# Two projection parts per attention unit, earlier exponentials, and a last residual kept in PSUM: a two-layer hybrid decoder trunk

## The chip, the cores and the metric

The kernel runs on one core of one Trainium2 chip. A core has five engines that run their own queues in order: TensorE (PE) for matrix products, VectorE (DVE), ScalarE (ACT), GpSimd (POOL) and SyncE (SP), which here only issues transfers. An engine that must wait for another stops at the waiting instruction, and everything behind it in its queue waits as well. The metric is the device time of one execution in microseconds; for several executions it is their median.

## The reference, cut to what matters

One sequence of 256 tokens, width 1024, all in float32. Layer 0 is a gated DeltaNet, layer 1 a sparse attention with three branches (compressed, selection, window), and each ends in a residual sum and a LayerNorm:

```
x  = layer_norm(alpha * x + gated_deltanet(x))          # layer 0
kv = six key/value projections of x, two of them compressed by a small MLP
q, z, gates = x @ b_w_in                                # 1024 + 3072 + 48 columns
o  = sum over 3 branches of gate * softmax(q k^T) v * silu(z)    # 16 heads of 64
x  = layer_norm(alpha * x + o @ b_w_out)                # layer 1, the output
```

With 256 tokens all blocks are selected and the window covers everything, so the selection and window branches are two causal softmaxes over 256 keys, and the compressed branch is one over 15 blocks.

## The kernel before, in words

All weights stream from HBM as tiles of 128x1024 into a ring of five raw buffers. ACT casts each one to a rounded high half (`hi_...`, L181) and POOL takes the difference as a low half (`lo_...`, L185); eight pairs can be held. A product is then three matmuls: high times high, high times low, low times high (L233 to L235). A **part** is six such matmuls of 512 columns: one weight tile against one half of the tokens (t = 0 or 1). Parts of the z projection write `pbz`, those of the output projection `pbo` (tokens 0 to 127) and `pbl` (tokens 128 to 255).

The order on PE, DVE, ACT and POOL is the order in which the Python code writes the instructions. Parts stand in a list `fills`, and `fill(n)` writes the next n of them. `defer(k, f)` puts work off until `step()` has been called k times; each `fill` of one part calls `step()` first. When the fourth part of a group of 512 z columns is written, its follow-up is deferred by one step: a tanh on ACT (`th`, L1236), then the multiplication with z on DVE (`zz<-th,pbz`, L1237). `get` and `presplit` write the casts of tiles that will be needed later.

The attention is a loop over 24 **units**, numbered 0 to 23 here. A unit of t = 0 is two heads for tokens 0 to 127; a unit of t = 1 is one head for tokens 128 to 255. The string `UNITS` gives their order. Each pass writes, in this order: `scores` (four matmuls into one of two PSUM tiles `s`), `maxima` (DVE adds the mask and reduces: L1345 to L1347 for t = 0, L1349 to L1352 for t = 1), `probs` of the unit before (ACT copies its transposed exponentials out of PSUM: `PT`, L1385, and `PcT`, L1389), `FA[i]` parts, one pending `merge`, `presplit`, `exps` (ACT, L1365 and L1366, or L1369 and L1370), `readout` of the unit before (PE, L1404, L1407, L1410, into the one PSUM tile `op`), `FB[i]` parts, and `transposes` (PE, L1378, into the one PSUM tile `ptp`, and L1380). The follow-up of a readout, `total` (five DVE instructions, L1418 to L1422), is deferred by one step and writes the gated sum into `zz`. For a unit of t = 0, `maxima` stands ahead of `probs` and `step`:

```
        first = i < n and units[i][0] == 0 and not merges
        if first:
            maxima(units[i])
```

`merge` transposes finished sums (PE `tp_b`, L1436; ACT `x1h`, L1440; DVE `x1l`, L1441), after which parts of the output projection can be written. `gates` (one ACT instruction, four DVE instructions, L1310 to L1315) works in place in a PSUM tile that is one of the two buffers of `s`, and is deferred to the first unit. The queries are split and transposed ahead of the loop: `q_split` (ACT and DVE, L1047 and L1048), `q_post` (PE `qtp`, L1223) and a deferred ACT copy to `qT` (L1224); the last of these transposes uses the PSUM buffer of `ptp`.

At the end, `done` adds the residual for tokens 128 to 255 in four quarters of 256 columns (`ln_part`, L914 and L915) and `ln_affine` normalises: `ln_mean` on DVE and POOL (L921 to L923), two DVE instructions that subtract the mean and multiply by the weight (L939), two that scale and add the bias (L942), each followed by a store.

Of the kernel before, what the change touches and what calls it, by code (L numbers as in the profile page):

```python
# [13 lines left out]
ALU = mybir.AluOpType  # L14
# [7 lines left out]
SQRT2 = float((2.0 * 2) ** 0.25)  # L22
# [12 lines left out]

FIRST = (1, 2)

UNITS = "001010101101101101111111"
FA = "3113111011210212044211123"
FB = "0211121311122110212111000"  # L40

PRE, TAIL = 4, 2
NEG = -1e30
# [50 lines left out]
def trunk(ctx: ExitStack, tc: tile.TileContext, I: dict, out: bass.AP):  # L94
    nc = tc.nc
    V, S, G, PE = nc.vector, nc.scalar, nc.gpsimd, nc.tensor
# [7 lines left out]
    def defer(n, f):  # L104
        late.append([n, f])

    def step():
        for e in late:
            e[0] -= 1
        due = [e for e in late if e[0] <= 0]  # L110
        late[:] = [e for e in late if e[0] > 0]
        for _, f in due:
            f()
# [82 lines left out]
    def lower():  # L196
        while lows:
            lows.pop(0)()
# [42 lines left out]
    def presplit():  # L241
        oldest = next(i for i, n in enumerate(uses) if n)
        split_to(min(state["top"] + PRE, oldest + NSPL, state["s"] + 1))
        lower()

    def fill(n, low=True):
        for _ in range(n):
            step()
            if fills:
                fills.pop(0)()  # L250
            if low:
                lower()
# [25 lines left out]
    first = ring.tile([P, 1024], F32, tag="raw", name="raw_first", bufs=NRAW)  # L278
    raws[order[0]] = first
    state["l"] = 1  # L280
    for q in range(4):
        if q in FIRST:
            c = slice(FIRST.index(q) * 512, FIRST.index(q) * 512 + 512)
# [48 lines left out]
    for q in range(5):  # L332
        if q < 4:
            c = slice(2 * q, 2 * q + 2)
# [223 lines left out]
    lo, hi = slice(0, 64), slice(64, 128)  # L558
# [233 lines left out]
    lnp = {}  # L792
# [115 lines left out]
    def ln_part(t, w, lo, ps, xin, dst):  # L908

        if lo == 0:  # L910
            stt[w, t] = [sm.tile([P, 4, 6], F32, tag="st", name=f"st_{w}{t}"), 0]
        st, n = stt[w, t]
        cc = slice(lo, lo + ps.shape[-1])
        V.scalar_tensor_tensor(dst[:, cc], xin[:, cc], SQRT2, ps, op0=ALU.mult, op1=ALU.add)  # L914
        V.bn_stats(st[:, n, :], dst[:, cc])  # L915
        stt[w, t][1] += 1

    def ln_mean(t, w):
# [6 lines left out]

    def ln_affine(t, w, b, dst, store=None, src=None):
        mv = ln_mean(t, w)
        if src:

            for c in range(2):  # L930
                V.scalar_tensor_tensor(src[c], src[c], mv[:, 0:1], lnp[w][:, c * 512:c * 512 + 512],
                                       op0=ALU.subtract, op1=ALU.mult)
            for c in range(2):
                cc = slice(c * 512, (c + 1) * 512)
                V.scalar_tensor_tensor(dst[:, cc], src[c], mv[:, 1:2], lnp[b][:, cc], op0=ALU.mult, op1=ALU.add)
            return
        for c in range(2):
            cc = slice(c * 512, (c + 1) * 512)
            V.scalar_tensor_tensor(dst[:, cc], dst[:, cc], mv[:, 0:1], lnp[w][:, cc], op0=ALU.subtract, op1=ALU.mult)  # L939
        for c in range(2):  # L940
            cc = slice(c * 512, (c + 1) * 512)
            V.scalar_tensor_tensor(dst[:, cc], dst[:, cc], mv[:, 1:2], lnp[b][:, cc], op0=ALU.mult, op1=ALU.add)  # L942
            if store:
                store(cc)

    def ln_affine_aside(t, w, b, dst, store):

        mv = ln_mean(t, w)
        nb = sm.tile([P, 1], F32, tag="nb", name=f"nb_{w}{t}")
        V.scalar_tensor_tensor(nb, mv[:, 0:1], -1.0, mv[:, 1:2], op0=ALU.mult, op1=ALU.mult)  # L950

        def half(c):
            cc = slice(c * 512, (c + 1) * 512)
            S.activation(dst[:, cc], dst[:, cc], AF.Identity, bias=nb, scale=mv[:, 1:2])
            G.tensor_tensor(dst[:, cc], dst[:, cc], lnp[w][:, cc], op=ALU.mult)
            G.tensor_tensor(dst[:, cc], dst[:, cc], lnp[b][:, cc], op=ALU.add)
            store(cc)

        defer(1, lambda: half(0))
        defer(3, lambda: half(1))  # L960
# [171 lines left out]
    for a in range(2):  # L1132
        for gp in range(2):
            step()
            ps = proj_fm(("skv", 2 * a + gp), x1h, x1l, f"pc{a}{gp}")
# [122 lines left out]
    add_pairs(48)  # L1258
    S.copy(wgs[:, :, 0:48], wg)
    G.tensor_tensor(wgs[:, :, 48:96], wg, wgs[:, :, 0:48].bitcast(F32), op=ALU.subtract)  # L1260
    fill(1)
    r = q_split()
    fill(1)
    compressed_v()
    for i in range(4):
        if i:
# [8 lines left out]
    for c in range(6):  # L1275
        for t in range(2):
            k = len(fills)
# [44 lines left out]
    order1 = [(1, h) for h in range(16)]  # L1322
    units = [order0.pop(0) if k == "0" else order1.pop(0) for k in UNITS]
    S_, PT_, PTT, PC, PCT, MX, TP = {}, {}, {}, {}, {}, {}, {}
# [29 lines left out]
    def exps(u):  # L1354
        t, h = u
        sp, mx = S_[u], MX[u]
        s4 = sp[:, :, 0:256].rearrange("p j (b k) -> p j b k", b=2)
        pt = PT_[u] = wk.tile([P, 2, 2, P], F32, tag="hl", name=f"pt{t}{h}", bufs=3)
        if t == 0 or h % 2 == 0:
            PC[t, h] = wk.tile([P, 2, 16], F32, tag="Pc", name=f"Pc{t}{h}", bufs=4)  # L1360
        Pc = PC[t, h - h % 2]
        if t == 0:
            for j in range(2):
                for b in range(2):
                    S.activation(pt[:, j, b, :], s4[:, j, b, :], AF.Exp, bias=mx[:, 2 * j + b:2 * j + b + 1])  # L1365
                S.activation(Pc[:, j, :], sp[:, j, 256:272], AF.Exp, bias=mx[:, 4 + j:5 + j])  # L1366
        else:
            for b in range(2):
                S.activation(pt[:, :, b, :], s4[:, :, b, :], AF.Exp, bias=mx[:, b:b + 1])  # L1369
            S.activation(Pc[:, h % 2, :], sp[:, 0, 256:272], AF.Exp, bias=mx[:, 4:5])  # L1370
# [11 lines left out]
    def probs(u):  # L1382
        t, h = u
        PT = PTT[u] = wk.tile([P, 2, 2, P], F32, tag="ra", name=f"PT{t}{h}", bufs=6)
        S.copy(PT.rearrange("p a b c -> p (a b c)"), TP[u])  # L1385
        if t == 0 or h % 2:
            h -= h % 2 * t
            PCT[t, h] = pct[len(PCT) % 2]
            S.copy(PCT[t, h][0:32, :], S_[u][0:32, 1, 272:400])  # L1389
# [39 lines left out]
    pb_ = {}  # L1429
# [13 lines left out]
    def bo_unit(t, c, part):  # L1443
        if part == 0:
            pb_[t, c] = [(sbank(f"pbl{c}{f}")[:, 0] if c else pjb(f"pbl{c}{f}")) for f in range(2)] if t else pjb(f"pbo{c}{t}")
        if t == 0 and c == 1 and part == 1:
            for nm in ("blw", "blb"):
                load_ln(nm, ring.tile([P, D], F32, tag="raw", name=nm, bufs=NRAW))
        x = x1[:, t, :]

        def store(cc):
            nc.sync.dma_start(out[t * P:(t + 1) * P, cc], x[:, cc])

        def done(lo, ps):
            ln_part(t, "blw", lo, ps, x, x)
            if lo + ps.shape[-1] == D:
                (ln_affine if t else ln_affine_aside)(t, "blw", "blb", x, store)

        if t == 1:

            for f in range(2):
                ps = pb_[t, c][f][:, 0:256]
                tm_part(ps, ("bo", 4 * c + part), part, t, *bT, cols=slice(256 * f, 256 * f + 256))
                if part == 3:
                    done(512 * c + 256 * f, ps)
            return
        tm_part(pb_[t, c], ("bo", 4 * c + part), part, t, *bT)
        if part == 3:
            defer(1, lambda: done(512 * c, pb_[t, c]))
# [5 lines left out]
    merges, ready = [], []  # L1475
    cnt["t0"] = 0

    def advance():
        if merges:
            merges.pop(0)()  # L1480
# [13 lines left out]
    n = len(units)  # L1494
    for i in range(n + 1):
        if i < n:
            scores(units[i])
        first = i < n and units[i][0] == 0 and not merges
        if first:

            maxima(units[i])
        if i:
            probs(units[i - 1])
        step()
        if i < n and not first:
            maxima(units[i])
        fill(int(FA[i]))
        advance()
        presplit()
        if i < n:  # L1510
            exps(units[i])
        if i:
            t, h = units[i - 1]
            if t == 0:
                readout(t, h)
                if h == 14:
                    cnt["t0"] = 1
                    merges += [lambda: merge0(0), lambda: merge0(1)] + ready
            else:

                if (units[i - 2] if h % 2 else units[i]) == (1, h ^ 1):
                    readout(t, h - h % 2, h % 2)
                elif h % 2:
                    readout(t, h - 1)
                if h % 4 == 3:
                    (merges if cnt["t0"] else ready).append(lambda g_=h // 4: merge1(g_))
        fill(int(FB[i]))
        if i < n:
            transposes(units[i])
# [79 lines left out]
```

## Time and profile before

| | |
|---|---|
| median of 3 runs | 386.9 us (386.45 to 387.45) |
| profiled execution, its own time | 388.53 us |
| profiled execution, span from first to last instruction | 386.8 us |
| PE busy | 374.7 us, 97% of the span |
| DVE, ACT, POOL busy | 58%, 57%, 64% |
| matrix products end at | about 379 us |

The profiled execution took 1.7 us more than its span and 1.6 us more than the median of the runs. Times in rows count from the start of the span. A row of a timeline gives the start, the length, the engine, the line, the operation, the output and inputs, the shapes, how many instructions it stands for, and in brackets how long the engine had been idle and on whom it waited. A matmul's length overlaps that of the next one, so the work of PE is read from the distance between two starts.

### The profile page before, as it was taken

The numbers are of one execution on the slowest core, as the hardware profiler recorded it, in microseconds if no ns is written. First come the engines' busy times: TensorE is split into PE (matmuls) and PEld (weight loads), VectorE is DVE, ScalarE is ACT, GpSimd is POOL, SyncE is SP. The second block draws the span as 40 slices with busy tenths as digits, with TensorE's granted clock in tenths as the row PEclk, the third lists the DMA queues.
The fourth block names the chain that finished last, engine by engine and source line by source line (L and its number), as shares of the span: only waits on it lengthen the run. The fifth ranks groups of instructions, "written<-read, shape, count | busy, mean of one in ns | idle before, by whom it ended". The sixth has DMA issues, their size and how long they took to land.

```text
span 386.8 us, 7558 instructions
## 1 busy us (share of the span) xinstructions
PE 374.7 (97%) x2870; PEld 332.9 (86%) x2870; DVE 223.6 (58%) x591; ACT 220.4 (57%) x433; POOL 247.1 (64%) x157
## 2 busy tenths in 40 slices
PE   8899999999999999999999999999999999999991
PEld 6899999999888987888897878888888888878991
DVE  2777876588642543656542545754557456677726
ACT  4687785546854543535563567675664757456410
POOL 5499999837456747895854997474736547209051
PEclk9999999999999999999999999999999999999997
DMA  6776749845433316384545854433516143301011
GB/s 223 292 218 208 268 158 297 228 167 143 148 109 112 110 54 200 128 287 147 169 158 166 297 195 159 164 111 109 173 45 218 55 153 113 117 3 54 3 54 54
DMA packets 23476, 58.68 MB, mean 152 GB/s; under 512 B 6672, under 2 KB 9232, under 8 KB 23312
## 3 DMA queue, kind: packets, MB, share of 16 engines
q1 hardware_dynamic: 23232, 58.13, 45.1%
q8 instruction: 22, 0.36, 0.4%
q14 instruction: 14, 0.11, 0.1%
q10 hardware_dynamic: 144, 0.07, 0.1%
q0 software_dynamic: 64, 0.01, 0.0%
HBM read 55.96 MB, written 2.23 MB: 150 GB/s over the span
## 4 chain that ended last, share of the span: by engine, by line
PE 90%; DMA 3%; DVE 2%; POOL 1%; ACT 1%; issue 1%; POOLq 0%; SPq 0%; DVEq 0%
PE pbz L235 6%; PE pbz L233 6%; PE pbz L234 6%; PE op L1407 4%; PE s L1336 3%; PE ptp L1378 3%; PE pwz L233 2%; PE pk L217 2%; PE pwo L235 2%; PE pq L216 2%; PE pq L215 2%; PE pq L217 2%; PE pk L215 2%; PE pk L216 2%; PE pwo L234 2%; PE pwo L233 2%
## 5 line engine op out<-in xcount | busy, mean ns | idle before, releaser
L185 POOL TENSOR_TENSOR lo_bz<-raw_bz,hi_bz 128x1024 fp32r<-128x1024 f32 x24 | 56.8, 2392 | 36.2 <-ACT hi_bz L181 19.6
L185 POOL TENSOR_TENSOR lo_wqkv<-raw_wqkv,hi_wqkv 128x1024 fp32r<-128x1024 f32 x22 | 52.5, 2406 | 7.9 <-ACT hi_wqkv L181 6.1
L233 PE MATMUL pbz<-hi_bz,x1h 128*128 128x512 f32 x96 | 38.7, 403 | 0.0
L235 PE MATMUL pbz<-lo_bz,x1h 128*128 128x512 f32 x96 | 37.8, 394 | 0.0
L234 PE MATMUL pbz<-hi_bz,x1l 128*128 128x512 f32 x96 | 37.6, 392 | 0.0
L185 POOL TENSOR_TENSOR lo_bo<-raw_bo,hi_bo 128x1024 fp32r<-128x1024 f32 x8 | 18.9, 2387 | 21.7 <-ACT hi_bo L181 16.9
L185 POOL TENSOR_TENSOR lo_skv<-raw_skv,hi_skv 128x1024 fp32r<-128x1024 f32 x12 | 28.4, 2397 | 4.2 <-PE pskv L235 4.2
L185 POOL TENSOR_TENSOR lo_wz<-raw_wz,hi_wz 128x1024 fp32r<-128x1024 f32 x8 | 19.4, 2438 | 16.0 <-ACT hi_wz L181 10.6
L181 ACT CAST hi_bz<-raw_bz 128x1024 fp32r<-128x1024 f32 x24 | 25.3, 1052 | 2.5 <-POOL wgs L1260 1.6
L185 POOL TENSOR_TENSOR lo_bq<-raw_bq,hi_bq 128x1024 fp32r<-128x1024 f32 x8 | 19.1, 2393 | 11.6 <-ACT hi_bq L181 7.2
L185 POOL TENSOR_TENSOR lo_wo<-raw_wo,hi_wo 128x1024 fp32r<-128x1024 f32 x8 | 18.9, 2385 | 11.9 <-ACT hi_wo L181 11.9
L1385 ACT COPY PT<-ptp 128x512 f32<-128x512 f32 x24 | 14.1, 588 | 21.2 <-PE ptp L1378 21.2
L181 ACT CAST hi_wqkv<-raw_wqkv 128x1024 fp32r<-128x1024 f32 x22 | 22.8, 1043 | 2.4 <-DMA raw_wqkv<-in_wqkv 2.4
L235 PEld LDWEIGHTS pbz<-lo_bz,x1h 128*128 128x128 f32 x96 | 18.0, 188 | 4.3 <-POOL lo_bz L185 0.2
L234 PEld LDWEIGHTS pbz<-hi_bz,x1l 128*128 128x128 f32 x96 | 18.1, 188 | 2.8
L233 PEld LDWEIGHTS pbz<-hi_bz,x1h 128*128 128x128 f32 x96 | 18.1, 188 | 2.8
L1369 ACT ACTIVATE pt<-s,mx 128x256 f32<-128x256 f32 x32 | 13.4, 471 | 10.9 <-DVE mx L1352 8.7
L217 PE MATMUL pk<-xh,lo_wqkv 128*128 128x256 f32 x64 | 18.2, 285 | 0.9 <-POOL lo_wqkv L185 0.9
L215 PE MATMUL pk<-xh,hi_wqkv 128*128 128x256 f32 x64 | 18.6, 290 | 0.0
L215 PE MATMUL pq<-xh,hi_wqkv 128*128 128x256 f32 x64 | 18.5, 289 | 0.0
L216 PE MATMUL pk<-xl,hi_wqkv 128*128 128x256 f32 x64 | 18.1, 283 | 0.0
L217 PE MATMUL pq<-xh,lo_wqkv 128*128 128x256 f32 x64 | 18.1, 283 | 0.0
(362 smaller groups left out, 1257.9 us busy)
## 6 DMA issues: line engine op xcount, KB each, us to landing
raw_bz<-in_bz SPq DMA_DIRECT2D x24, 512.0 KB, 3.3
raw_wqkv<-in_wqkv SPq DMA_DIRECT2D x23, 512.0 KB, 4.4
raw_skv<-in_skv SPq DMA_DIRECT2D x12, 512.0 KB, 3.3
raw_wz<-in_wz SPq DMA_DIRECT2D x8, 512.0 KB, 3.9
raw_wo<-in_wo SPq DMA_DIRECT2D x8, 512.0 KB, 3.6
raw_bq<-in_bq SPq DMA_DIRECT2D x8, 512.0 KB, 3.6
raw_bo<-in_bo SPq DMA_DIRECT2D x8, 512.0 KB, 3.3
raw_w<-in_w SPq DMA_DIRECT2D x4, 512.0 KB, 3.3
```

What stands on the lines that cost most here:

```text
L181: S.copy(h, r)
L185: e.tensor_tensor(l, r, h.bitcast(F32), op=ALU.subtract)
L215: PE.matmul(ps[:, 0:T], wh[:, kt, :], ah[:, kt, :], start=kt == 0, stop=False)
L216: PE.matmul(ps[:, 0:T], wh[:, kt, :], al_[:, kt, :], start=False, stop=False)
L217: PE.matmul(ps[:, 0:T], wl[:, kt, :], ah[:, kt, :], start=False, stop=kt == 7)
L233: PE.matmul(ps, ah[:, kt, tt], wh[:, k4, cols], start=kt == 0, stop=False)
L234: PE.matmul(ps, al_[:, kt, tt], wh[:, k4, cols], start=False, stop=False)
L235: PE.matmul(ps, ah[:, kt, tt], wl[:, k4, cols], start=False, stop=kt == 7)
L1336: PE.matmul(sp[:, j, 0:n], lq, kk[:, hh // 4, c0:c0 + n], start=i == 0, stop=i == 1)
L1369: S.activation(pt[:, :, b, :], s4[:, :, b, :], AF.Exp, bias=mx[:, b:b + 1])
L1385: S.copy(PT.rearrange("p a b c -> p (a b c)"), TP[u])
L1407: PE.matmul(o3[:, r, 1 + b, :], PT[:, j, b, :], vt_[:, b, j, g_, :], start=j == 0, stop=j == 1)
```

## The change

The tables that order the units and place the parts are rewritten: every unit has one part behind its scores and one behind its readout almost everywhere, where before some had none and some four. For units of t = 0 the exponentials are now written right behind `probs`, ahead of `step()`. For the others they are written ahead of `presplit`. Where a merge is pending, one of the parts behind the scores is now written after the merge. `q_split` for the first group of queries stands one part earlier. In the last LayerNorm the residual sums of columns 0 to 511 stay in PSUM, so the first pass has three instructions, two of 256 columns that read PSUM and one of 512.

```diff
-UNITS = "001010101101101101111111"
-FA = "3113111011210212044211123"
-FB = "0211121311122110212111000"
+UNITS = "001101100111011100111111"
+FA = "3112121111111111111222223"
+FB = "0111111111111111101001000"
...
-        V.scalar_tensor_tensor(dst[:, cc], xin[:, cc], SQRT2, ps, op0=ALU.mult, op1=ALU.add)
-        V.bn_stats(st[:, n, :], dst[:, cc])
+        y = ps if dst is None else dst[:, cc]
+        V.scalar_tensor_tensor(y, xin[:, cc], SQRT2, ps, op0=ALU.mult, op1=ALU.add)
+        V.bn_stats(st[:, n, :], y)
...
-        for c in range(2):
-            cc = slice(c * 512, (c + 1) * 512)
-            V.scalar_tensor_tensor(dst[:, cc], dst[:, cc], mv[:, 0:1], lnp[w][:, cc], op0=ALU.subtract, op1=ALU.mult)
+        for c, y in enumerate(src):
+            cc = slice(c * 256, (c + 1) * 256)
+            V.scalar_tensor_tensor(dst[:, cc], y, mv[:, 0:1], lnp[w][:, cc], op0=ALU.subtract, op1=ALU.mult)
+        cc = slice(512, 1024)
+        V.scalar_tensor_tensor(dst[:, cc], dst[:, cc], mv[:, 0:1], lnp[w][:, cc], op0=ALU.subtract, op1=ALU.mult)
...
-    fill(1)
     r = q_split()
-    fill(1)
+    fill(2)
...
+            inb = t == 1 and lo < 512
+            ln_part(t, "blw", lo, ps, x, None if inb else x)
...
+        if first:
+            exps(units[i])
         step()
         if i < n and not first:
             maxima(units[i])
-        fill(int(FA[i]))
+
+        k = 1 if merges else 0
+        fill(int(FA[i]) - k)
         advance()
+        fill(k)
+        if i < n and not first:
+            exps(units[i])
         presplit()
-        if i < n:
-            exps(units[i])
```

Three places show how instructions move. In the names, digits behind `s`, `mx`, `pt`, `op` are t and the head (`pt014` is t = 0, heads 14 and 15), those behind `th` and `pbz` are the group of columns and t. The lines of the changed kernel are two or three higher.

ACT at unit 0, before:

```order
L181 CAST hi_bz_6_3049<-raw_bz_6_2908 128x1024
L1224 CAST qT1_2696<-qtp110_3059 128x4x128
L1224 CAST qT1_2696<-qtp111_3064 128x4x128
L1310 ACT_TABLE_LOAD
L1310 ACTIVATE gq_3069<-gq_3069 128x96
L181 CAST hi_bz_7_3090<-raw_bz_7_2935 128x1024
L1236 ACTIVATE th00_3101<-pbz00_3004 128x512
L1365 ACTIVATE pt00_3117<-s00_3072,mx00_3077 128x128 x2
```

The same place on ACT in the changed kernel:

```order
L181 CAST hi_bz_6_3049<-raw_bz_6_2908 128x1024
L1367 ACT_TABLE_LOAD
L1367 ACTIVATE pt00_3081<-s00_3072,mx00_3077 128x128 x2
L1368 ACTIVATE Pc00_3082<-s00_3072,mx00_3077 128x16
L1367 ACTIVATE pt00_3081<-s00_3072,mx00_3077 128x128 x2
L1368 ACTIVATE Pc00_3082<-s00_3072,mx00_3077 128x16
L1227 CAST qT1_2696<-qtp110_3059 128x4x128
L1227 CAST qT1_2696<-qtp111_3064 128x4x128
L1312 ACTIVATE gq_3069<-gq_3069 128x96
```

The table load and the exponentials of unit 0 moved ahead of the last two query copies and of the gates.

DVE around the last unit of t = 0 (heads 14 and 15), before, where it is unit 16:

```order
L1237 SCALAR_TENSOR_TENSOR zz3_3808<-th41_3993,pbz41_3896 128x512
L1345 TENSOR_TENSOR s014_4030<-s014_4030,cb_2284 128x2x272
L1346 TENSOR_REDUCE mx014_4035<-s014_4030 128x4
L1347 TENSOR_REDUCE mx014_4035<-s014_4030 128x2
L1418 RECIPROCAL op16_4014<-op16_4014 128x6
```

The same on DVE in the changed kernel, where it is unit 17, from the maxima of unit 16 on:

```order
L1347 TENSOR_TENSOR s012_3962<-s012_3962,cb_2284 128x2x272
L1348 TENSOR_REDUCE mx012_3967<-s012_3962 128x4
L1349 TENSOR_REDUCE mx012_3967<-s012_3962 128x2
L1240 SCALAR_TENSOR_TENSOR zz1_3560<-th50_3982,pbz50_3878 128x512
L1420 RECIPROCAL op18_3945<-op18_3945 128x6
L1421 TENSOR_TENSOR rc18_4003<-op18_3945,gt_2977 128x6
L1422 TENSOR_TENSOR op18_3945<-op18_3945,zz3_3869 128x6x64
L1423 TENSOR_TENSOR op18_3945<-op18_3945,rc18_4003 128x6x64
L1424 TENSOR_REDUCE zz3_3869<-op18_3945 128x128
L1347 TENSOR_TENSOR s014_4021<-s014_4021,cb_2284 128x2x272
```

A total of unit 16, and the multiplication with z ahead of it, now stand in front of the maxima of unit 17.

ACT at the second merge of t = 0, before:

```order
L1385 COPY PT110_4167<-ptp110_4157 128x512
L1440 CAST x1h_2043<-tp_b04_4174 128x4x128
L1369 ACTIVATE pt111_4181<-s111_4162,mx111_4169 128x2x128 x2
L1370 ACTIVATE Pc110_4137<-s111_4162,mx111_4169 128x16
L181 CAST hi_bo_4_4191<-raw_bo_4_3922 128x1024
```

The same merge on ACT in the changed kernel, in unit 20:

```order
L1387 COPY PT111_4185<-ptp111_4174 128x512
L1391 COPY PcT1_2389<-s111_4134 32x128
L1442 CAST x1h_2043<-tp_b04_4199 128x4x128
L1239 ACTIVATE th51_4206<-pbz51_4116 128x512
L181 CAST hi_bo_4_4210<-raw_bo_4_3992 128x1024
L1371 ACTIVATE pt112_4220<-s112_4180,mx112_4188 128x2x128 x2
```

A tanh and a cast moved ahead of the exponentials.

## Rows read from the trace of the kernel before

**Rows 1.** The page: busy time of the engines, share of the span and instructions

```profile
PE 374.7 (97%) x2870; PEld 332.9 (86%) x2870; DVE 223.6 (58%) x591; ACT 220.4 (57%) x433; POOL 247.1 (64%) x157
```

**Rows 2.** Timeline of PE and ACT where the first queries are transposed

```profile
222.23 0.39 PE L234 MATMUL pbq<-hi_bq,x1l 128*128 128x512 f32 x1
222.46 0.39 PE L235 MATMUL pbq<-lo_bq,x1h 128*128 128x512 f32 x1
223.38 0.66 PE L1223 MATMUL qtp<-ident,hlq 128*128 128x128 f32 x4 [0.54 <-DVE hlq L1048]
...
221.55 1.06 ACT L181 CAST hi_bz<-raw_bz 128x1024 fp32r<-128x1024 f32 x1 [1.56 <-POOL wgs L1260]
```

**Rows 3.** Timeline of PE at the merges: transposes of unit 17, then the next output part

```profile
337.56 0.91 PE L1378 MATMUL ptp<-ident,pt 128*128 128x128 f32 x4
...
343.54 0.66 PE L1436 MATMUL tp_b<-ident,zz 128*128 128x128 f32 x4 [0.19 <-ACT PT L1385]
...
345.51 0.48 PE L233 MATMUL pbo<-hi_bo,x1h 128*128 128x512 f32 x1
```

**Rows 4.** Timeline of PE in unit 1, and the first maximum of unit 2

```profile
247.41 1.00 PE L1404 MATMUL op<-vtok,PT 128*128 128x65 f32 x8
...
248.25 0.44 PE L1410 MATMUL op<-vbd,PcT 128*128 128x130 f32 x2
...
251.30 0.60 PE L1378 MATMUL ptp<-ident,pt 128*128 128x128 f32 x4
...
251.77 0.37 PE L1336 MATMUL s<-kh,qT 128*128 128x272 f32 x1
...
252.53 0.43 DVE L1349 TENSOR_TENSOR s<-s,cb 128x256 f32<-128x256 f32 x1 [1.01 <-PE s L1336]
```

**Rows 5.** Timeline of DVE, ACT and PE in units 16 and 7 of t = 0

```profile
331.14 0.73 DVE L1345 TENSOR_TENSOR s<-s,cb 128x544 f32<-128x544 f32 x1 [3.01 <-PE s L1336]
...
332.81 0.62 ACT L1365 ACTIVATE pt<-s,mx 128x128 f32<-128x128 f32 x2 [1.59 <-DVE op L1418]
...
334.33 0.28 PE L1380 MATMUL s<-ident,Pc 128*32 128x128 f32 x1
...
285.30 0.63 ACT L1236 ACTIVATE th<-pbz 128x512 f32<-128x512 f32 x1
...
285.96 0.69 DVE L1237 SCALAR_TENSOR_TENSOR zz<-th,pbz 128x512 f32<-128x512 f32 x1 [2.11 <-ACT th L1236]
```

**Rows 6.** Timeline of DVE: the first and the last of the five instructions of a total

```profile
273.57 0.20 DVE L1418 RECIPROCAL op<-op 128x6 f32<-128x6 f32 x1 [1.83 <-PE op L1410]
...
275.21 0.56 DVE L1422 TENSOR_REDUCE zz<-op 128x128 f32<-128x384 f32 x1
```

**Rows 7.** Timeline of ACT, DVE and PE at unit 0, and an earlier table load

```profile
239.68 1.07 ACT L1224 CAST qT<-qtp 128x512 fp32r<-128x512 f32 x2 [0.20 <-PE qtp L1223]
240.78 1.28 ACT L1310 ACT_TABLE_LOAD   x1
...
242.55 0.26 DVE L1311 TENSOR_SCALAR gq<-gq 128x96 f32<-128x96 f32 x1
...
243.93 0.24 DVE L1315 TENSOR_SCALAR gt<-gq,cb 128x16 f32<-128x16 f32 x1
...
244.98 0.60 PE L1378 MATMUL ptp<-ident,pt 128*128 128x128 f32 x4
...
20.01 1.28 ACT L471 ACT_TABLE_LOAD   x1 [0.54 <-DVE cv L465]
```

**Rows 8.** Instructions of L922 and L923 (ns min/median/max, first and last start), timeline of DVE

```profile
L922 POOL TENSOR_SCALAR mv_blw<-mv_blw x2: 222/500/778, 366.5 to 380.4; 128x1 f32<-128x1 f32 x2
...
L923 POOL TENSOR_TENSOR mv_blw<-mv_blw,mhalf x2: 572/748/925, 366.8 to 381.3; 128x1 f32<-128x1 f32 x2
...
380.39 1.42 DVE L939 SCALAR_TENSOR_TENSOR x<-x,mv_blw,blw 128x512 f32<-128x512 f32 x2
382.26 1.42 DVE L942 SCALAR_TENSOR_TENSOR x<-x,mv_blw,blb 128x512 f32<-128x512 f32 x2 [0.46 <-POOL mv_blw L923]
```

More of the change, by code (lines that the diff above doesn't have):

```diff
@@ L927, in ln_affine @@
         mv = ln_mean(t, w)
-        if src:
+        if src and not store:
             for c in range(2):
@@ L1454, in done @@
         def done(lo, ps):
-            ln_part(t, "blw", lo, ps, x, x)
+            inb = t == 1 and lo < 512
+            ln_part(t, "blw", lo, ps, x, None if inb else x)
             if lo + ps.shape[-1] == D:
-                (ln_affine if t else ln_affine_aside)(t, "blw", "blb", x, store)
+                if t:
+                    ln_affine(t, "blw", "blb", x, store, [p[:, 0:256] for p in pb_[1, 0]])
+                else:
+                    ln_affine_aside(t, "blw", "blb", x, store)
         if t == 1:
```

## The prediction

> **What bounds the kernel now.** The page comes first: PE is busy for 374.7 of 386.8 us [rows 1], so the others matter only where PE waits for them, and after its last matmul. Next come the distances between starts on PE in the stages that the change touches, because modelled ends hide waits. A matmul of 512 columns follows the one before by 0.23 us [rows 2], so a part of six is 1.38 us. Wherever PE's distances equal this work, nothing can be won; three places are longer. At the first transposes of queries PE stands until DVE has split them [rows 2]. At the merges, the stretch from the transposes of unit 17 to the next output part is 7.95 us [rows 3]. After the matmuls come the residual sums and the last normalisation, where DVE waits 0.46 us for POOL [rows 8]. All else that PE does in these stages is the same before and after, since the change only reorders it.
>
> **What it removes.**
> Queries: the split waits in ACT's queue behind a cast of 1.06 us that itself waits for POOL [rows 2]. After the change it stands ahead of that cast. Without the wait the transposes would start at 222.46 + 0.23 = 222.69 instead of 223.38: 0.69 us. The profile calls 0.54 of it idle; I take 0.69, and 0.54 is the lower bound.
>
> Merges: the work in those 7.95 us is two sets of transposes (0.47 and 0.44), two of scores (0.58 each), two merges of four transposes (0.44 each), and readouts of 16, 2 and 8 matmuls (1.68, 0.28, 0.84). These lengths come from unit 1: eight matmuls of a readout 0.84, transposes and the small one behind them 0.47, a readout with its last pair and two parts 3.89, which leaves 0.28 for the pair [rows 4]; scores are what remains of 244.98 to 247.41 after 0.47 and a part [rows 7, 4]. The sum is 5.75, so 2.2 us are waits: no part stood there to cover the totals and copies. In the changed kernel a part stands ahead of each merge and one behind it. With some tenths at single transposes around it I take 2.5, between 1.5 and 2.7.
>
> Last normalisation: the two small POOL instructions took 778 and 925 ns there, and 222 and 572 ns at the other call [rows 8], 0.91 more. DVE was then working through L939, whose operands are all in SBUF; after the change its first two instructions read PSUM. L939 to L942 is 1.87 us; two instructions of 256 columns and one of 512 need about 1.5, and POOL's 0.8 fits inside. So at most 0.4 is won; an extra instruction and sums written to PSUM may eat most of it, so 0.1 is the other end. I take 0.25.
> [...]
>
> Removed in all: 0.69 + 2.5 + 0.25 = 3.4 us.
>
> **What it adds: waits of PE behind the new orders.** A time zero at the start of a unit's scores makes them easy to add. Scores last 0.58, and the maxima start at 0.76 [rows 4]. For t = 0 the exponentials follow 1.67 after the maxima and take about 1.5; the small transpose behind the big ones starts 3.19 after the maxima, and there PE had to wait [rows 5].
>
> Unit 0: the first exponentials now bring the table load. In the trace it ran at 240.78 in ACT's idle time. It now waits for the maxima, which end near 242.6 (DVE starts its next instruction at 242.55) [rows 7]; at 20.01 a load shows such a wait for DVE, and takes 1.28 [rows 7]. So: 242.6 + 1.28 + 1.5 = 245.4. Behind this in ACT's queue stand the last two copies of queries, 1.07 for both [rows 7], to 246.45, and the second of them frees the PSUM buffer of the unit's transposes. These start at about 246.5 instead of 244.98. Next in the queue are the gates: 0.2 on ACT, then four DVE instructions, 1.62 from 242.55 to 244.17 [rows 7], to 248.3. They work in the buffer that unit 1's scores need. Those scores would have started at 244.98 + 0.47 = 245.45; they start at 248.3. Together PE loses 2.8 us. If the load is hidden after all it is 1.5, the lower bound.
> [...] The row at 240.78, 0.03 us behind the copies, shows the load alone.
>
> Units 16 and 17: both are t = 0. Unit 16 has one part, a readout with its pair, and a part: next scores at 0.58 + 3.89 + 0.47 = 4.94. On ACT its exponentials end at 0.76 + 1.67 + 1.5 = 3.93, the tanh of a finished group is behind them, and the multiplication with z follows 0.66 later on DVE and takes 0.69 [rows 5]: 5.28. Behind it stands the total, 2.20 from first to last [rows 6]: 7.48. The maxima of unit 17 are next on DVE; due at 5.70, they are 1.8 late. Its small transpose can start at 7.48 + 3.19 = 10.67. PE would be there at 4.94 + 0.58 + 1.38 + 0.84 + 0.28 + 0.44 = 8.46, since unit 17 has no part behind its readout. Wait: 2.2, and 2.0 after the overlap that neighbours on one engine show.
>
> Unit 18: two casts (1.06 each) now stand between unit 17's exponentials and the copy of its transposes. These end near 10.65 + 2.1 + 0.6 = 13.4, and PE wants them at 10.7 + 0.58 + 1.38 = 12.66. By the sum 0.7; I take 0.55, and 0 if the casts come later.
>
> Unit 9: unit 8 has the pattern of unit 16, so its total ends at 7.48, and only then is the PSUM tile of the readout free. PE wants it at 4.94 + 0.58 + 1.38 = 6.9. By the sum 0.6, with overlap 0.4.
>
> Unit 20: a tanh (0.63) and a cast (1.06) now stand between the merge's copy and the exponentials [rows 5, 2]. Nothing to 1.7; PE has about a microsecond of other work there, so I take 0.7.
>
> Units 2, 10 and 12: the multiplication with z stands ahead of their maxima, or cover is short (two parts in unit 12). 0.1 to 0.2 each, 0.4 together, from 0 to 1.0.
>
> Added: 2.8 + 2.0 + 0.55 + 0.4 + 0.7 + 0.4 = 6.85 us.
>
> The sum is 6.85 - 3.45 = 3.4, rounded down to 3.3 since overlaps shorten most terms. Against the profiled execution's own 388.53 us that is 391.8. That execution was 1.6 above the median of the runs, so for the median I add it to 386.9: **390.2 us**. A difference within 0.3%, 1.2 us, counts as no change here.
>
> **Rivals.**
> Cover is enough (faster). A readout and two parts, 3.89 us, now lie between nearly all scores and their transposes, and unit 2's maxima started on time behind such a unit [rows 4]. If units 0 and 17 wait no more than that, only gains and small losses remain: 386.9 - 3.4 + 0.5 = 384.0. It decides at a total of 2.3 us of new waits. Against it: the queues are in order, and ACT and DVE have the work of [rows 5 to 7] in front of what PE needs.
>
> The table load doesn't wait (no change). If it runs early, as at 240.78, and the late totals overlap more than I allow, unit 0 costs 1.5 and unit 17 1.5, the rest 1.5: 4.5 - 3.4 = +1.1, so 388.0.
>
> [...]
>
> The half in PSUM brings nothing: +0.25, 390.5, inside the forecast.
>
> **How the numbers follow.** The forecast with its neighbours above 388.1: 0.70, of which the drain has 0.06. No change, at 386 to 388: 0.18. Cover is enough: 0.12. Bounds of the terms give 4.0 to 9.0 added and 2.1 to 3.8 removed. Both at their ends are unlikely, so the forecast alone reaches from 388.1 to 392.0. The range takes in the no-change case and leaves out the faster one and the far end: 386.0 to 392.0.
>
> **What would show it.** The table load at unit 0 behind DVE, copies of queries behind the exponentials, and PE idle for some 1.4 us ahead of the first `ptp` and 1.3 ahead of the second `s`. About 2 us of PE idle at the transposes of heads 14 and 15. The first `qtp` straight behind its part. No idle time ahead of `tp_b`. L922 and L923 at the end near 222 and 572 ns. The forecast is wrong if unit 0's load lies ahead of the maxima, or if `total` of unit 16 ends before unit 17's scores.

## The result, and the profile after

| | before | after |
|---|---|---|
| median | 387.0 us (6 runs, 386.45 to 387.51) | 391.6 us (6 runs, 390.38 to 392.53) |
| profiled execution, own time and span | 388.53, 386.8 us | 392.0, 390.0 us |

The ratio of after to before is 1.0113, 95% interval 1.0091 to 1.0135: the change makes the kernel 4.5 us slower. The prediction said 390.2 us, slower, in a range from 386.0, which takes in no change, to 392.0.

The page of the changed kernel, the line that answers to [rows 1]. The busy times hardly differ, so the new time is waiting, or the same work done more slowly.

```profile
PE 375.9 (96%) x2870; PEld 333.3 (85%) x2870; DVE 223.1 (57%) x592; ACT 219.2 (56%) x433; POOL 246.5 (63%) x157
```

The waits of PE by who ended them (total, times, longest, all in us), changed kernel:

```profile
PE ptp L1380 <- ACT qT L1227: 1.4, 1, 1.4
PE s L1338 <- DVE gt L1317: 1.1, 1, 1.1
...
PE op L1406 <- DVE zz L1424: 0.8, 2, 0.4
PE ptp L1380 <- ACT pt L1367: 0.5, 1, 0.5
```

Of these the trace of before has only a wait of `op` for `zz`, at the merges, 0.6 us in two; the two here are in units 9 and 17. The timeline of the changed kernel, ACT, DVE, PE and POOL, at unit 0 and unit 1 (it answers to [rows 7] and [rows 4]; the first queries, for [rows 2], stand ahead of it, and the last normalisation, for [rows 8], behind it):

```profile
221.05 0.39 PE L235 MATMUL pbq<-lo_bq,x1h 128*128 128x512 f32 x1
221.28 0.60 PE L1226 MATMUL qtp<-ident,hlq 128*128 128x128 f32 x4
...
240.56 1.28 ACT L1367 ACT_TABLE_LOAD   x1 [3.23 <-DVE mx L1349]
241.85 0.63 ACT L1367 ACTIVATE pt<-s,mx 128x128 f32<-128x128 f32 x2
...
243.19 1.11 ACT L1227 CAST qT<-qtp 128x512 fp32r<-128x512 f32 x2
244.13 0.30 ACT L1312 ACTIVATE gq<-gq 128x96 f32<-128x96 f32 x1
...
245.86 0.24 DVE L1317 TENSOR_SCALAR gt<-gq,cb 128x16 f32<-128x16 f32 x1
...
242.60 0.39 PE L235 MATMUL pbz<-lo_bz,x1h 128*128 128x512 f32 x1
244.34 0.66 PE L1380 MATMUL ptp<-ident,pt 128*128 128x128 f32 x4 [1.35 <-ACT qT L1227]
...
246.24 0.36 PE L1338 MATMUL s<-kh,qT 128*128 128x272 f32 x1 [1.13 <-DVE gt L1317]
...
247.07 0.63 PE L233 MATMUL pbz<-hi_bz,x1h 128*128 128x512 f32 x1
247.50 0.63 PE L234 MATMUL pbz<-hi_bz,x1l 128*128 128x512 f32 x1
...
249.63 1.14 PE L1406 MATMUL op<-vtok,PT 128*128 128x65 f32 x8
...
383.92 0.88 DVE L940 SCALAR_TENSOR_TENSOR x<-pbl,mv_blw,blw 128x256 f32<-128x256 f32 x2
...
385.37 1.41 DVE L945 SCALAR_TENSOR_TENSOR x<-x,mv_blw,blb 128x512 f32<-128x512 f32 x2
...
383.97 0.22 POOL L923 TENSOR_SCALAR mv_blw<-mv_blw 128x1 f32<-128x1 f32 x1 [6.71 <-DVE mv_blw L922]
384.27 0.57 POOL L924 TENSOR_TENSOR mv_blw<-mv_blw,mhalf 128x1 f32<-128x1 f32 x1
```

The reader is to follow the queue on ACT: the table load waits for the maxima, the exponentials for the load, the copies of queries for the exponentials, the gates for the copies. ACT stands idle for 3.23 us ahead of the load; the copies start at 243.19, though the transposes that they read ran from 236.88 on:

```profile
236.88 1.04 PE L1226 MATMUL qtp<-ident,hlq 128*128 128x128 f32 x8
```

PE's first wait is 244.34 - (242.60 + 0.23) = 1.51 us; its second 246.24 - (244.34 + 0.47) = 1.43 us. Behind them something else: the matmuls of the next part start 0.43 us apart, not 0.23. The windows of the same execution (busy time of each engine, then PEclk, the granted clock as a share of full speed, DMA share and GB/s):

```profile
246.00:247.00 1.00, 0.76 (x4) 0.79 (x5) 0.68 (x2) 0.43 (x2) 1.00 (x1) 0.75 0.00 0
247.00:248.00 1.00, 1.00 (x5) 0.81 (x4) 0.69 (x1) 0.00 (x0) 0.83 (x1) 0.50 0.00 0
248.00:249.00 1.00, 1.00 (x4) 0.81 (x3) 0.83 (x3) 0.02 (x1) 0.00 (x0) 0.50 0.42 49
249.00:250.00 1.00, 1.00 (x5) 0.81 (x5) 0.00 (x0) 1.00 (x5) 0.00 (x0) 0.55 0.76 279
```

The granted clock is at 0.50 instead of 1.00 from about 246.5 to 249.9. From unit 1's scores to its readout it takes 249.63 - 246.24 = 3.39 us. In before it was 247.41 - 245.45 = 1.96, with the end from [rows 4] and the start from this row:

```profile
245.45 0.37 PE L1336 MATMUL s<-kh,qT 128*128 128x272 f32 x1
```

That is 1.4 us more.

### The profile page after: what moved, and what is told of

It is laid out like the page before. It is cut to its first block, busy times and chain, and to the rows that moved or that the text cites. A ratio compares the mean times of both kernels' runs of the same rounds, so it can differ in the third digit from the quotient of the medians.

```text
span 390.0 us, 7551 instructions
## 1 busy us (share of the span) xinstructions
PE 375.9 (96%) x2870; PEld 333.3 (85%) x2870; DVE 223.1 (57%) x592; ACT 219.2 (56%) x433; POOL 246.5 (63%) x157
## 5 line engine op out<-in xcount | busy, mean ns | idle before, releaser
L233 PE MATMUL pbz<-hi_bz,x1h 128*128 128x512 f32 x96 | 39.8, 415 | 0.0
L216 PE MATMUL pq<-xl,hi_wqkv 128*128 128x256 f32 x64 | 18.1, 283 | 0.0
```

What stands on the lines that cost most here:

```text
L216: PE.matmul(ps[:, 0:T], wh[:, kt, :], al_[:, kt, :], start=False, stop=False)
L233: PE.matmul(ps, ah[:, kt, tt], wh[:, k4, cols], start=kt == 0, stop=False)
```

## The experiments

Medians and intervals of the ratio are against the kernel before in executions on the same chip. Where kernels are compared with each other, it is by their medians; those of before in the different batches were 387.0 to 387.4 us, so such a difference can be off by some 0.4. Where traces are compared, it is by what PE takes from the last matmul ahead of the first `qtp` to its last matmul of all: 156.2 us in before, 161.1 in after.

**late0**, to see what unit 0's exponentials cost by themselves:

```diff
-        if first:
+        if first and i:
             exps(units[i])
...
-        if i < n and not first:
+        if i < n and not (first and i):
             exps(units[i])
```

> The changed kernel, with unit 0's exponentials alone written where the kernel before had them (behind unit 0's three parts); tables, all other early exponentials, the split of queries and the last LayerNorm stay changed. Theory A (the exponentials with the table load, ahead of the last two copies of queries and of the gates, cause both waits of PE, 1.5 and 1.4 us, and the fall of the granted clock from 1.00 to 0.50 that follows them, another 1.4 us): both waits and the stretch at 0.50 are gone, the first ptp starts about 0.43 behind its last part, unit 1's scores right behind it; 391.6 - 4.4 = 387.2 us. Rival B (the fall of the clock has nothing to do with the waits and comes in these executions anyway): 391.6 - 3.0 = 388.6, with a stretch at 0.50 left between 240 and 260. Rival C (the early position is needed and the wait only moves to unit 0's or unit 1's transposes): 390 or more.

Measured: 387.9 us, ratio 1.0025 (1.0006 to 1.0044). The place of unit 0's exponentials is worth 3.7 us. In its trace PE waits neither ahead of the first `ptp` nor ahead of unit 1's scores, and PEclk is 1.00 between 240 and 260. The median lies between A and B; in the traces PE takes 157.0 us, 4.1 less than in after, close to the 4.4 of theory A. One of the twelve executions took 392.1 us at a mean granted clock of 0.988, although unit 0's waits are gone; no trace shows why.

**before_early0**, the opposite: this place alone, in the kernel before:

```diff
             probs(units[i - 1])
+        if first and not i:
+            exps(units[i])
         step()
...
-        if i < n:
+        if i < n and not (first and not i):
             exps(units[i])
```

> The kernel before, with one edit: unit 0's exponentials written ahead of its step, as in the changed kernel. Theory A (this edit alone brings the two waits of 2.9 us and a stretch at a granted clock of 0.50 behind them that costs 1.4): 387.0 + 4.3 = 391.3 us, with PE waiting ahead of the first ptp and of unit 1's scores and PEclk near 0.8 between 240 and 250. Rival B (waits without the clock): 389.9. Rival C (the waits need the new tables too): under 388.

Measured: 390.8 us, ratio 1.0101 (1.0080 to 1.0122), between A and B. Rival C falls: the waits need no new tables. Timeline of PE in this kernel, the first queries and then units 0 and 1:

```profile
221.21 0.39 PE L235 MATMUL pbq<-lo_bq,x1h 128*128 128x512 f32 x1
221.51 0.66 PE L1223 MATMUL qtp<-ident,hlq 128*128 128x128 f32 x4
...
242.85 0.39 PE L235 MATMUL pbz<-lo_bz,x1h 128*128 128x512 f32 x1
244.59 0.66 PE L1378 MATMUL ptp<-ident,pt 128*128 128x128 f32 x4 [1.35 <-ACT qT L1224]
...
246.49 0.36 PE L1336 MATMUL s<-kh,qT 128*128 128x272 f32 x1 [1.14 <-DVE gt L1315]
...
247.06 0.39 PE L233 MATMUL pbz<-hi_bz,x1h 128*128 128x512 f32 x1
247.29 0.40 PE L234 MATMUL pbz<-hi_bz,x1l 128*128 128x512 f32 x1
...
248.45 1.00 PE L1404 MATMUL op<-vtok,PT 128*128 128x65 f32 x8
```

The waits are those of after to 0.02 us, yet here the matmuls behind them are 0.23 apart: in this execution the clock did not fall, PEclk is 1.00 from 240 to 260. Its span is 387.8 us; the other five are 388.3, 389.0, 389.1, 390.4 and 390.7. The waits come from the order of the queues, so I take them to be in every execution, though only one was traced. The fall of the clock is not in this one; the longest, 390.7, has the lowest mean clock, 0.988.

**early0_filled**, to see whether the idle time makes the clock fall. PE gets matmuls with zeros in both waits; they add nothing to the result:

```diff
+    def idle_fill(n):
+        for _ in range(n):
+            PE.matmul(state["ps"], zr, x1h[:, 0:2, :].rearrange("p a b -> p (a b)"), start=False, stop=False)
...
         fill(int(FB[i]))
+        if i == 0:
+            idle_fill(6)
         if i < n:
             transposes(units[i])
+        if i == 0:
+            idle_fill(6)
```

> The kernel before_early0 (unit 0's exponentials early in the kernel before; 390.75 us, with single executions from 389.5 to 392.4) with both waits of PE filled: six matmuls of 512 columns with zeros, added to the z columns under way, ahead of unit 0's transposes and six ahead of unit 1's scores, 1.4 us each. They depend on nothing late, so the waits end when they did before. Theory A (the granted clock falls to 0.50 in some executions because PE stands in these two waits): with PE working through them it never falls there; the waits themselves stay paid, so 387.1 + 3.0 = 390.1 us, single executions within 389.3 to 390.9, none above. Rival B (the clock falls for another reason): single executions still up to 392 and a median of 390.7. Rival C (the zeros themselves delay what follows, by a matmul or two at each place): 390.5 with no execution near 389.6.

Measured: 389.95 us, single executions from 389.44 to 390.19, where before_early0 had 389.54 to 392.41; ratio 1.0060 (1.0037 to 1.0083). That is 2.8 us above before, the two waits alone. Timeline of PE:

```profile
243.22 1.56 PE L1293 MATMUL pbz<-x1h,zr 128*128 128x512 f32 x6
244.76 0.66 PE L1386 MATMUL ptp<-ident,pt 128*128 128x128 f32 x4
...
245.28 1.65 PE L1293 MATMUL pbz<-x1h,zr 128*128 128x512 f32 x6
```

Every one of six executions stayed low, against three of six above 390.8 without the zeros, and in the profiled one PEclk is 1.00 from 240 to 260. Both ends moved as theory A has it, but six against six is not many. Rival B is not out either: among the eleven executions of before in the same batch, which have none of these waits, one took 389.49 us at a mean clock of 0.990, and the others at most 388.29.

**preload**, to take the table load alone out of the chain:

```diff
+    ed = sm.tile([P, 1], F32, tag="ed", name="ed", bufs=1)
+    S.activation(ed, cb[:, C_ROW:C_ROW + 1], AF.Exp)
     gq = sbank("gq")[:, 0, :]
```

> The changed kernel with one added instruction: an exponential of one column of constants on ACT, ahead of unit 0, so that the table load need not wait for unit 0's maxima; nothing else moves. Theory A (of the 2.9 us at unit 0 the load behind the maxima is 1.28, as the prediction's lower bound of 1.5 had it, and the rest is the order of exponentials, copies and gates): the first ptp waits about 0.2 instead of 1.5 us, unit 1's scores still 1.4, 391.6 - 1.3 = 390.3; a stretch at a granted clock of 0.50 may stay behind the second wait, and without it 389. Rival B (the load finds another place for itself or is hidden): 391.6.

Measured: 389.8 us, ratio 1.0069 (1.0047 to 1.0090), 1.8 less than after. The load runs at 237.40, ahead of the maxima; the first `ptp` starts 0.24 later than its part would let it, and unit 1's scores still wait 1.14: theory A. In this profiled execution the clock stayed up at unit 0 (PEclk 1.00 from 240 to 250) and fell at unit 17, where PE had waited 0.38 us ahead of `op`, 0.50 ahead of `ptp`, and again between the transposes of the two heads. The matmuls of the part behind start 0.42 and 0.43 us apart (335.47, 335.89, 336.32). Windows of it:

```profile
333.00:336.00 3.00, 2.75 (x11) 2.22 (x12) 2.01 (x5) 3.00 (x9) 0.78 (x1) 0.69 0.40 143
336.00:338.00 2.00, 2.00 (x9) 1.60 (x7) 1.17 (x4) 1.35 (x5) 2.00 (x2) 0.62 0.01 4
338.00:342.00 4.00, 4.00 (x28) 3.56 (x27) 3.00 (x7) 2.35 (x5) 4.00 (x2) 1.00 0.64 203
```

**cover17**, for the wait at unit 17: a part is moved there from unit 15.

```diff
-FB = "0111111111111111101001000"
+FB = "0111111111111110111001000"
```

> The changed kernel, with one part moved from behind the readout in unit 15 to behind the readout in unit 17 (one digit of the table FB each). Theory A (PE waits for the late maxima of unit 17 only because too little work stands ahead of its transposes): of the 1.95 us lost there 1.4 to 1.6 go, unit 15 waits some 0.3, and the copy of unit 17's transposes changes little: 391.6 - 1.2 = 390.4 us, with the wait ahead of ptp of unit 17 at 0.5 us or less. Rival B (DVE's chain of z, total and maxima is the bound, so that cover only moves the wait to units 18 and 19): 391.2 to 391.6, with the 0.2 ahead of op in unit 18 grown to 1 us or more.

Measured: 390.4 us, ratio 1.0081 (1.0063 to 1.0098), 1.1 less than after: theory A. The wait ahead of unit 17's `ptp` is gone from the trace. Unit 0's two waits, which this edit leaves, are there with 1.36 and 1.13 us of idle time, and the clock fell behind them as in after: the matmuls of the next part start 0.42 and 0.43 us apart (248.35, 248.77, 249.20), and the window has a PEclk of 0.84:

```profile
240.00:250.00 10.00, 7.51 (x31) 5.90 (x30) 4.98 (x11) 5.86 (x14) 4.50 (x2) 0.84 0.35 116
```

**late0_cover17**, both edits:

> Both of the edits before on the changed kernel: unit 0's exponentials late, and the part moved from unit 15 to unit 17. Theory A (the two costs are apart and add): 391.6 - 4.4 - 1.2 = 386.0 us, a little faster than the kernel before (386.9). Theory A with other costs unaccounted for (what the prediction took as gains, 3.4 us, is smaller than it was taken): the same, since the measured times of after already hold them. Rival (they do not add, because the later units are bound by ACT and DVE, not by when they start): 387 or more.

Measured: 386.7 us, ratio 0.9986 (0.9975 to 0.9997). The two measured costs add: 3.7 + 1.1 = 4.8, and 391.6 - 4.8 = 386.8. The 386.0 of theory A was too low, as its 4.4 for unit 0 was too much in the median.

**late_all**, all exponentials back behind `presplit`:

```diff
-        if first:
-            exps(units[i])
...
-        if i < n and not first:
-            exps(units[i])
         presplit()
+        if i < n:
+            exps(units[i])
```

> The changed kernel with all exponentials where the kernel before had them: behind the parts, the merge and presplit in every unit (unit 0 too). To be compared with late0 (387.9 us), where only unit 0's are late. Theory A (the early place pays for the other units: with a tanh of 0.6 or a cast of 1.05 ahead of the exponentials the transposes of several units wait, 0.5 us or more each): 389 to 391. Rival B (a readout and two parts cover the difference, so that the new place brings nothing outside unit 0): 387.5 to 388.3.

Measured: 385.7 us, ratio 0.9962 (0.9949 to 0.9975). Both expectations were wrong: outside unit 0 the early place is neither a gain nor worth nothing, it costs another 2.2 us there.

**late_t0**, to find which of the two moved places:

```diff
-        if first:
-            exps(units[i])
...
-        if i < n and not first:
+        if i < n:
             exps(units[i])
```

> The changed kernel with the exponentials of t = 0 units alone written late, behind the parts; both kinds then stand ahead of presplit. Compared with late_all (385.7 us, all behind presplit) and late0 (387.9, only unit 0 late). Theory A (what the early place costs outside unit 0 is that exponentials which wait for the maxima hold up a tanh on ACT, and behind it the multiplication with z, the total and the next maxima on DVE; a place ahead of presplit costs nothing): 385.7, within 0.4. Rival B (the casts of presplit that now come behind the exponentials are as much to blame, as in the prediction's term for unit 18): half of the difference or more, 386.5 to 388.

Measured: 385.4 us, ratio 0.9951 (0.9935 to 0.9966): theory A. The place ahead of `presplit` costs nothing that shows; that of t = 0 ahead of `step` costs it all. Against late0, 387.9 - 385.4 = 2.5 us come off in the median and 157.0 - 154.4 = 2.6 on PE. The timeline of the changed kernel at units 16 and 17, which answers to [rows 5, 6]:

```profile
329.41 0.44 PE L1412 MATMUL op<-vbd,PcT 128*128 128x130 f32 x2
...
331.55 0.37 PE L1338 MATMUL s<-kh,qT 128*128 128x272 f32 x1
...
334.06 1.08 PE L1406 MATMUL op<-vtok,PT 128*128 128x65 f32 x8 [0.36 <-DVE zz L1424]
...
335.91 1.27 PE L1380 MATMUL ptp<-ident,pt 128*128 128x128 f32 x4 [0.50 <-ACT pt L1367]
...
337.06 0.37 PE L1338 MATMUL s<-kh,qT 128*128 128x272 f32 x1
...
329.13 0.63 ACT L1367 ACTIVATE pt<-s,mx 128x128 f32<-128x128 f32 x2 [1.57 <-DVE mx L1349]
...
330.45 0.63 ACT L1239 ACTIVATE th<-pbz 128x512 f32<-128x512 f32 x1
...
331.12 0.69 DVE L1240 SCALAR_TENSOR_TENSOR zz<-th,pbz 128x512 f32<-128x512 f32 x1 [2.11 <-ACT th L1239]
331.73 0.20 DVE L1420 RECIPROCAL op<-op 128x6 f32<-128x6 f32 x1
...
333.83 0.72 DVE L1347 TENSOR_TENSOR s<-s,cb 128x544 f32<-128x544 f32 x1
```

And the same places in late_t0:

```profile
324.99 0.44 PE L1412 MATMUL op<-vbd,PcT 128*128 128x130 f32 x2
...
322.98 0.58 ACT L1239 ACTIVATE th<-pbz 128x512 f32<-128x512 f32 x1
324.70 0.63 ACT L1367 ACTIVATE pt<-s,mx 128x128 f32<-128x128 f32 x2 [1.13 <-DVE mx L1349]
...
324.50 0.68 DVE L1240 SCALAR_TENSOR_TENSOR zz<-th,pbz 128x512 f32<-128x512 f32 x1
325.46 0.20 DVE L1420 RECIPROCAL op<-op 128x6 f32<-128x6 f32 x1 [0.29 <-PE op L1412]
...
327.91 0.73 DVE L1347 TENSOR_TENSOR s<-s,cb 128x544 f32<-128x544 f32 x1 [0.25 <-PE s L1338]
```

In after the exponentials stand first on ACT, idle for 1.57 us until the maxima are there, and the tanh, whose z columns are long done, stands behind them. Then z, the total and the maxima of unit 17 are late in turn: the total starts 331.73 - 329.41 = 2.3 us behind the readout's last pair. In late_t0 the tanh runs in that idle time, z follows the maxima at once, and the total starts 0.5 us behind its pair. From scores to scores unit 17 then takes 4.03 us instead of 5.51; the work is 3.52, so 0.5 of the 2.0 stays.

**late_all_cover17**, both edits of late_all and cover17:

> All exponentials late, and one part moved from behind the readout in unit 15 to behind the readout in unit 17. In the trace of late_all PE still loses about 0.9 us at unit 17's transposes (0.26 ahead of them, 0.68 at the small one). Theory A (it is cover that is missing there): 385.7 - 0.7 = 385.0 us. Rival B (unit 15, which gives the part, waits as long): 385.7 or more.

Measured: 386.8 us, ratio 0.9984 (0.9969 to 0.9999). No gain, as rival B had it, but not for its reason: unit 15 does not wait. In the trace the 0.9 us at unit 17's transposes are gone and 0.55 has come ahead of unit 17's `op`. PE takes 154.9 us in either kernel, and the median span is 384.0 in both. The median time is above late_all's by 1.1 because the executions took 1.8 to 3.2 us more than their spans, where late_all's took 1.7; why is open.

**no_behind**, late0_cover17 without a part between merge and readout:

```diff
-        k = 1 if merges else 0
+        k = 0
```

> The kernel late0_cover17 (386.7 us) with one edit: all parts of a unit with a merge are written ahead of the merge, none between the merge and the readout. Theory A (the part behind a merge is what covers the copy of its transposes on ACT, 0.6 us, and the exponentials that queue behind that copy): PE waits about 0.5 to 1.1 us at the transposes of the next unit at each of the four or five merges without a part behind the readout: 386.7 + 2 to 4 = 389 to 391. Rival B (what counts is only that parts are left at all for the units with merges, not where they stand): 386.7 to 387.5.

Measured: 388.8 us, ratio 1.0039 (1.0024 to 1.0053), 2.1 above late0_cover17: theory A. Waits of PE in the stretch with the merges, none of which late0_cover17 has:

```profile
PE ptp L1380 <- ACT pt L1371: 0.7, 1, 0.7
PE ptp L1380 <- DVE op L1420: 0.5, 1, 0.5
...
```

**before_q**, the moved split of queries alone in the kernel before, and **before_ln**, the last normalisation alone:

```diff
-    fill(1)
     r = q_split()
-    fill(1)
+    fill(2)
```

> The kernel before with one edit: the first q_split one part earlier, ahead of both parts. Theory A (the 0.69 us that PE stood there comes off the end, since PE has no slack behind it): 387.3 - 0.7 = 386.6 us, ratio 0.998, and the first qtp straight behind its part. Rival B (the gain is given back at the next place where PE waits for ACT or the merges): 387.3, ratio 1.000.

Measured: 386.9 us, ratio 0.9993 (0.9983 to 1.0003): less than can be told from nothing, and 0.7 is at the edge of the interval. In its trace the first `qtp` does follow its part by 0.24 us, and PE takes 155.4 us instead of 156.2 (before), or 156.0 (before_ln, where `qtp` follows by 0.75). But before_early0 keeps the old order of queries too, and there `qtp` follows its part by 221.51 - 221.21 = 0.30: the wait that this edit takes away is long in some executions and hardly there in others.

```diff
-        V.scalar_tensor_tensor(dst[:, cc], xin[:, cc], SQRT2, ps, op0=ALU.mult, op1=ALU.add)
+        y = ps if dst is None else dst[:, cc]
+        V.scalar_tensor_tensor(y, xin[:, cc], SQRT2, ps, op0=ALU.mult, op1=ALU.add)
...
+            inb = t == 1 and lo < 512
+            ln_part(t, "blw", lo, ps, x, None if inb else x)
...
```

> The kernel before with one edit: the last residual's columns 0 to 511 stay in their banks. Theory A (while DVE reads a bank, the two small POOL instructions take 222 and 572 ns instead of 778 and 925; DVE reaches the scaling 0.42 us earlier, as in the changed kernel): 387.3 - 0.4 = 386.9 us, ratio 0.999. Rival B (sums written to banks are slower by as much, as the lower bound of the prediction's term had it): -0.1 us.

Measured: 386.7 us, ratio 0.9992 (0.9980 to 1.0004). The median moved by the 0.4 of theory A, but the interval holds no change as well as this gain; on this measurement alone nothing is shown.

## Why the prediction was right, and where it fell short

The direction and its mechanism were right: in-order queues on ACT and DVE put work that waits ahead of work that PE needs, as at unit 0, where ACT stood 3.23 us ahead of the load with the copies of queries behind it.

**Unit 0, predicted 2.8.** 1.51 + 1.43 = 2.9 us in the trace of after, by the chain as predicted. preload takes 1.3 of it away at the first `ptp`, the length of the load: the lower bound of 1.5 was the rest. The prediction gives 0.06 of its chances to a drain, time lost behind the load; no run shows one: the load takes 1.28 us, and ACT's next instruction starts 0.01 us behind it in after and in before, 0.02 us in preload.

**What was left out.** The sum counted waits as time lost and nothing behind them. The fall of the clock adds 1.4 us in the profiled execution. PE takes 382.17 - 221.05 = 161.1 us there, against 156.2 in before; without the 1.4 that is 3.5 more, where the prediction's terms for this stretch give 6.85 - 0.69 - 2.5 = 3.7. So between these two traces the sum of the terms holds, and the clock came on top. That the profiled execution's own time, 392.0, is still close to the 391.8 of the sum is luck: before's profiled execution ended the part ahead of the first `qtp` 1.4 us later than after's (222.46 against 221.05); in before_early0 it is at 221.21.

**The median, 1.4 above the forecast.** This is explained only in part. The six spans of after are 388.7, 388.8 and 388.8, and 389.8, 390.0 and 390.2; the median spans of before in the batches of the experiments are 385.3 to 385.6, so the lower three stand 3.1 to 3.5 above them, which is about the predicted 3.3. The two at 390.0 and 390.2 have a mean clock of 0.991, and the first is the one whose trace shows the fall; all executions of before in the batches of the experiments but one have 0.992 to 0.997. (The mean also holds the time behind the last matmul, which is at 0.50 from 382.0 to 386.8 in before's trace and from 386.5 to 390.0 in after's.) But the two executions that the median rests on show no low clock: one, with a span of 389.8, has 0.996, and the other has a span of only 388.8 and took 2.9 us more than it, where most took 1.7. So the clock can account for the two longest spans, one of them traced, and not for all of the 1.4; a part of it may be the term for the queries, which was taken too large, as said below.

**Units 16 and 17, predicted 2.0.** From scores to scores 337.06 - 331.55 = 5.51 us, for 3.52 of work (0.58 + 1.38 + 0.84 + 0.28 + 0.44): 2.0. **Unit 9, predicted 0.4:** 0.4 idle ahead of `op`, 0.6 by distances. **Unit 18, predicted 0.55:** 0.2 idle, 0.4 by distances. **Unit 20, predicted 0.7:** 0.5 by distances. **Units 2, 10 and 12, predicted 0.4:** 0.2 each at the transposes of 10 and 12, none in 2. The prediction had the chain of units 16 and 17 right, the tanh behind the exponentials among its links, and laid it to the two units' being neighbours with a z group between them. In late_t0 the units keep that order and most of the wait is gone, so the early exponentials ahead of the tanh are what counts: outside unit 0 they account for 2.5 us.

**Removed, predicted 3.4.** Merges: no idle time ahead of `tp_b` in after, and no_behind shows that the part behind a merge is worth 2.1 us where it stands. The gain of 2.5 by itself was not measured. An estimate: the waits found above add to 6.8 us by distances and the stretch grew by 3.5, so 3.3 went, of it 0.7 at the queries and 2.6 at the merges. late_t0, with all the gains and few of the waits, is 1.9 us below before. Last normalisation, predicted 0.25: the two POOL instructions (L923, L924 in after) took 0.22 and 0.57 us, and from the first pass to the second it is 385.37 - 383.92 = 1.45 us instead of 1.87. While they run DVE is at L940, which reads PSUM, and for the last 0.13 us (384.71 to 384.84) at L942, whose operands are in SBUF. Why they are shorter than the 0.78 and 0.93 us of before was not shown. In the median the gain is the 0.4 of before_ln, which can't be told from nothing.

Queries, predicted 0.69: this term was mis-sized, since it was read from one execution. In kernels that keep the old order the first `qtp` follows its part by 0.92 us (before), 0.75 (before_ln), 0.37 (early0_filled) and 0.30 (before_early0), where 0.23 is no wait. So the edit wins 0.1 to 0.7 us by execution; the prediction took the largest of these. In the median of before_q it is 0.2.

**The rivals.** Cover is enough: false for the change; late_t0, with ACT's queue free, gets 1.9 of the 2.9 us that this rival had, so the tables do cover most. The load doesn't wait: false, it starts at 240.56 and the maxima end at 240.46.

The fastest version of those tried is late_t0: 1.9 us faster than before, and 0.9951 / 1.0113 = 0.984 of after.

## What to carry to other kernels

An instruction put early in an in-order queue takes the whole queue to its own wait: before moving it up, list what stands behind it (here copies, gates and a tanh, behind 3.23 us of idle time on ACT at unit 0) and who waits for those. A wait of the matrix engine can cost more than its length: behind two waits it was 1.4 us more in after's profiled execution, at a granted clock of 0.50, and nothing in before_early0's, at 1.00. So places where waits stand close together are worth mending first, though it was not shown that their closeness decides. A wait that is read from one execution can be much shorter in the next (here 0.92 us from the part to the first `qtp` in one and 0.30 in another, where 0.23 is no wait), so read it in several traces before counting it as a gain. When a change holds gains and losses, undo one line at a time: here one condition on t = 0 units held all of the loss.

## What the runs showed of the hardware

In after's profiled execution the granted clock fell from 1.00 to 0.50 (PEclk of 247 to 249) behind two waits, 1.35 and 1.13 us of idle time with only the five transposes of unit 0 between them. In cover17's it fell behind the same two, of 1.36 and 1.13 us: PEclk is 0.84 from 240 to 250. With such waits in before_early0, of 1.35 and 1.14 us, it was 1.00 from 240 to 260 in the profiled execution. At 0.50 a part of six matmuls took 2.56 us in after (247.07 to 249.63) instead of 1.38. In preload the clock fell at unit 17 instead, behind idle times of 0.38 and 0.50 us and at a third wait between the transposes: PEclk is 0.69 from 333 to 336 and 0.62 from 336 to 338. In after, with idle times of 0.36 and 0.50 at the same place, it was 1.00 from 330 to 340. With zeros multiplied in unit 0's waits (early0_filled) it was 1.00 from 240 to 260 in the profiled execution, and the six executions took at most 390.19 us. Long executions at a low mean clock came once without unit 0's waits in late0 (392.1 us, 0.988) and once in before (389.49 us, 0.990). What decides between falling and not falling in one execution stays open.
